# A mixture-of-experts loop written as one fixed cycle per pair of experts

## The chip, the cores and the metric

The kernel is one program on one core of a Trainium2 chip. TensorE (PE) multiplies matrices and loads its stationary operand in a separate stage (PEld); VectorE (DVE), ScalarE (ACT) and GpSimd (POOL) do elementwise work; SyncE (SP) issues the weight transfers from DRAM, which 16 DMA engines carry out. SBUF is the on-chip store, PSUM holds matmul results. The metric is the device time of one execution in microseconds (us), as the median of several runs.

## The reference

Two transformer blocks over 256 tokens of width 1024. The first ends in a mixture of 32 experts; the second (adaptive norms, a Hyena long convolution beside differential attention, a feed-forward layer) is not touched by the change. The part that matters, cut down:

```python
def block_ffn(args):                       # one block of rows of one expert
    tok, e = args
    xb = xt[tok]
    hb = jax.nn.silu(xb @ w1[e]) * (xb @ w3[e])      # 1024 -> 512
    return hb @ w2[e]                                # 512 -> 1024
...
y = jnp.einsum('nk,nkd->nd', gate, y_assign)         # each token: 2 of 32 experts
```

The Hyena filters of the second block do not depend on the tokens: a small two-layer network with sines (f1, f2), its output layer times a decay (f3), and its Fourier transform (fH), for each of two orders n.

## The kernel before, in words

The tokens of each expert are gathered by a matmul with a 0/1 matrix: up to 64 tokens for an expert, two experts (a *pair*) side by side in 128 columns. `NJ` is 16 pairs. For pair j the loop (L1303 to L1332) makes these pieces of work, whose names and lines are those of the profile:

- `up(j, "w1")` and `up(j, "w3")` (L1266): 16 products each into a PSUM tile `hw`. A product is 64 rows of stationary tokens by 512 columns of weights; the two experts of a pair use the two halves of PE's columns ("half-column products"), alternating. The first 8 of 16 read kb 0 of the weight, the last 8 read kb 1.
- `act_half` (L1271): SiLU on ACT into `sg`; at L1325 DVE multiplies `sg` by the w3 result.
- `turn` (L1277): four 128x128 transposes of `sg` into `tp`, and ACT copies them to `hT` (L1279).
- `down(j)` (L1296): 16 half-column products of `hT` with w2, into `po0` and `po1`.
- `combine` (L1014): scales `po` by the gates and splits it in a high part `oth` (ACT, L237) and a low part `otl` (DVE, L238); eight full-width products `py` scatter the rows back to the tokens; DVE adds each of four results to `x` (L1016).
- `gather` (L936, L937): 8 blocks per group of two pairs, each of 4 products `pxg` and an ACT copy into `xg`; the loop takes 2 + 2 blocks in each pair up to pair 13.
- `hooks`: at pair 6 `filters` sets up the Hyena filter work, at pairs 7 to 14 one filter step each (f1, f2, f3(0), fH(0,0), fH(0,1), f3(1), fH(1,0), fH(1,1) with the inverse), at pair 15 `wide_ring`.

Each pair needs 12 weight loads of 1 MiB (4 of w1, 4 of w3, 4 of w2; L1231, the last w2 in halves at L1292), 192 MiB in all. SP issues them in program order into a ring of SBUF buffers (`wtile`): a load waits until the products of the load that had its buffer before are done. The ring has 16 buffers until pair 6. There `filters` gives ten of them up and adds two, so that 8 are left, after the w1 loads of pair 6; at pair 15 three are added.

In the code of before, the w3 products come in two parts: w3 kb 0, then `down(j-1)`, then two gather blocks, then w3 kb 1; `turn` of the pair before stands right behind w1. But the code's order is not the order on PE: a list scheduler of the language orders each engine's instructions by priority and by when it takes them to be ready, so that pieces of neighbouring steps are interleaved. PSUM holds three sets of tiles: `acc` has 4 tiles (`hw1`, `hw3`, `po0`, `po1`), `tp` two and `sm` two; `py` uses two of each, and before the change all gather blocks use `sm`.

Of the kernel before, what the change touches and what calls it, by code (L numbers as in the profile page):

```python
# [100 lines left out]

def _body(nc, tc, I, out, ctx, dbg):
    V, A, G, T = nc.vector, nc.scalar, nc.gpsimd, nc.tensor

    cst = ctx.enter_context(tc.tile_pool(name="cst", bufs=1))
    NA = 4
# [816 lines left out]
    def gather(iot, d1, d2, xg):  # L923


        hot = wk.tile([P, 2, 256], F32R, name="hot", tag="junk", bufs=1)
        for t in range(2):
            hit = wk.tile([P, S], F32, name="hit", tag="tb", bufs=1)
            V.tensor_scalar(hit, iot, d1[:, t:t + 1], None, op0=OP.is_equal)
            V.scalar_tensor_tensor(hot[:, t, :], iot, d2[:, t:t + 1], hit, op0=OP.is_equal, op1=OP.add)  # L930

        def block(k):
            p = smp("pxg")[:, :256]
            for t in range(2):
                for z_ in range(2):
                    T.matmul(p, xn[z_][:, t, k * P:(k + 1) * P], hot[:, t, :], start=t + z_ == 0, stop=t + z_ == 2)  # L936
# [50 lines left out]
    def bc_rows(dst, src):  # L987
        p = smp("prow")
        for k in range(2):
            for t in range(2):  # L990
                T.matmul(p[:, k * S + t * P:k * S + (t + 1) * P], src[:, k, t:t + 1].to_broadcast([P, P]), ident,
                         start=True, stop=True)
        V.tensor_copy(dst, p.rearrange("p (k s) -> p k s", k=2))

    def combine(rw, sid, po, done=None):

        ET = wk.tile([P, S], F32R, name="ET", tag="wh", bufs=4)
        tmp = wk.tile([P, S], F32, name="ETt", tag="tb", bufs=1)
        gs = mo.tile([P, 2], F32, name="gs", tag="gs", bufs=4)
        V.tensor_scalar(tmp, rw[:, 0, :], sid, None, op0=OP.is_equal)  # L1000
        V.scalar_tensor_tensor(ET, rw[:, 1, :], sid, tmp, op0=OP.is_equal, op1=OP.add)
        for k in range(2):
            V.scalar_tensor_tensor(tmp, rw[:, k, :], sid, rows[:, 1, k, :], op0=OP.is_equal, op1=OP.mult,
                                   accum_out=gs[:, k:k + 1])
        V.tensor_tensor(gs[:, 0:1], gs[:, 0:1], gs[:, 1:2], op=OP.add)
        hl = []
        for hf in range(2):
            hl.append([wk.tile([P, 512], F32R, name=n_, tag=g_, bufs=4) for n_, g_ in (("oth", "wh"), ("otl", "wl"))])
            hilo(*hl[hf], po[hf], gs[:, 0:1])
        for t in range(2):  # L1010
            for hf in range(2):
                p = smp("py") if t == 0 else tpp("py")
                for z_ in range(2):
                    T.matmul(p, ET[:, t * P:(t + 1) * P], hl[hf][z_], start=z_ == 0, stop=z_ == 1)  # L1014
# [13 lines left out]
    def overflow(n_over):  # L1028
        with tc.If(n_over > 0):  # L1029
# [34 lines left out]
            with tc.For_i(0, n_over, 1):  # L1064
# [17 lines left out]
                for st in range(2):  # L1082
                    A.activation(sgs[st], hps[0][st], AF.Silu)
                    V.tensor_tensor(sgs[st], sgs[st], hps[1][st], op=OP.mult)
                    p = tpp()
                    for q in range(4):
                        T.transpose(p[:, q * P:(q + 1) * P], sgs[st][:, q * P:(q + 1) * P], ident)
# [26 lines left out]
    def lambdas():  # L1114
        V.tensor_tensor(lv[:, 0:2, :], lv[:, 0:2, :], lv[:, 2:4, :], op=OP.mult)
        ls = mo.tile([1, 2], F32, name="ls")
        V.tensor_reduce(ls, lv[:, 0:2, :], AX.X, OP.add)
        A.activation(ls, ls, AF.Exp)
        V.scalar_tensor_tensor(ls[:, 0:1], ls[:, 0:1], 0.2, ls[:, 1:2], op0=OP.add, op1=OP.subtract)
        p = smp("lam")  # L1120
        T.matmul(p[:, 0:1], ones[0:1, :], ls[:, 0:1], start=True, stop=True)
        V.tensor_copy(lam, p[:, 0:1])

    def filters():
# [37 lines left out]
        def inverse():  # L1162

            hilo(*dfs, dft)
            for ri in range(2):
                p = tpp()
                for fb_ in range(2):
                    for t in range(2):
                        T.transpose(p[:, fb_ * S + t * P:fb_ * S + (t + 1) * P], dft[:, ri, t, fb_ * P:(fb_ + 1) * P], ident)
                A.activation(inv[:, ri], p.rearrange("p (b s) -> p b s", b=2), AF.Copy, scale=(1 - 2 * ri) / 256.0)  # L1170

        def f1():
            p = smp("f1")
            T.matmul(p[0:64, :S], w1, zT, start=True, stop=True)
            h1 = st["h1"] = fp.tile([64, S], F32, name="fh1")
            sin_of(h1, p[0:64, :S], fb[:, 0:1], fb[:, 2:3])

        def f2():
            p = smp("f2")
            T.matmul(p[0:64, :S], w2, st["h1"], start=True, stop=True)  # L1180
            h2 = st["h2"] = fp.tile([65, S], F32, name="fh2")
            sin_of(h2[0:64, :], p[0:64, :S], fb[:, 1:2], fb[:, 2:3])
            V.memset(h2[64:65, :], 1.0)

        def f3(n):
# [3 lines left out]
            for t in range(2):  # L1189
                for d_ in range(2):  # L1190
                    p = smp("f3")
                    T.matmul(p, st["h2"][:, t * P:(t + 1) * P], w3[:, d_ * 512:(d_ + 1) * 512], start=True, stop=True)
# [7 lines left out]
        def fH(n, ri):  # L1200
            src = st["src"][ri]
            for fb_ in range(2):
                p = smp("fH")
                for t in range(2):
                    T.matmul(p, dft[:, ri, t, fb_ * P:(fb_ + 1) * P], src[:, t, :], start=t == 0, stop=t == 1 and ri == 1)  # L1205
                if ri == 0:

                    for k in range(4):
                        T.matmul(p[:, k * P:(k + 1) * P], col["hy_bias_2"][:, 4 * n + k:4 * n + k + 1].to_broadcast([P, P]),
                                 ident, start=False, stop=k == 3)  # L1210
# [49 lines left out]
    def up(j, nm, hps, kbs):  # L1260
        s0 = (j % 2) * P
        for kb in kbs:
            we = [eload(nm, 2 * j + e, kb, 4, 512) for e in range(2)]
            for k in range(4):
                for e in range(2):
                    T.matmul(hps[64 * e:64 * e + 64, :], xgs[j][:, 4 * kb + k, s0 + 64 * e:s0 + 64 * e + 64], we[e][:, k, :],  # L1266
                             start=kb + k == 0, stop=kb + k == 4)

    def act_half(hps):
        sg = wk.tile([P, 512], F32, name="sg", tag="wl", bufs=4)  # L1270
# [3 lines left out]
    def turn(sg):  # L1274
        p = tpp()
        for q in range(4):
            T.transpose(p[:, q * P:(q + 1) * P], sg[:, q * P:(q + 1) * P], ident)  # L1277
# [4 lines left out]
    def down(j, hT):  # L1282
        po = [acc("po0"), acc("po1")]
        for kb in range(2):
# [8 lines left out]
            for q in range(2):  # L1293
                for hf in range(2):
                    for e in range(2):
                        T.matmul(po[hf][64 * e:64 * e + 64, :], hT[:, 2 * kb + q, 64 * e:64 * e + 64],  # L1296
                                 we[e][:, q, hf * 512:(hf + 1) * 512], start=kb + q == 0, stop=kb + q == 2)
# [6 lines left out]
    prev = None  # L1304
    for j in range(NJ):
        if j == 2:
            combine(rows[:, 0], slotc[:, 1:2], down(1, turn(prev)))
            prev = None
            overflow(n_over)
        if j % 2 == 0 and j + 2 < NJ:  # L1310
# [15 lines left out]
        if j == 0:  # L1326
            n_over = nc.values_load(novi[0:1, 0:1], min_val=0, max_val=7)
            bc_rows(rows[:, 0], dest)
            bc_rows(rows[:, 1], gt)
# [4 lines left out]
    combine(rows[:, 0], slotc[:, NJ - 1:NJ], down(NJ - 1, turn(prev)), norm_part)  # L1334
    tap("x3", x)
    moctx.close()

# [317 lines left out]
```

## Time and profile before

| | before |
|---|---|
| median of 3 runs | 1326.5 us (1323.0 to 1326.77) |
| the profiled execution, own time | 1325.16 us |
| its span (first to last instruction) | 1323.3 us |
| mean granted PE clock, share of full | 0.993 |
| PE busy | 1277.0 us (97%) |
| DVE, ACT, POOL busy | 747.7, 552.6, 69.3 us |
| the expert stage, from its first weights to the last `po` | about 388 to 880 us of the span |

Busy means that an instruction of that engine is under way; for PE the ends are modelled, and a wait for the weights inside a row of products is not always seen as idle. DMA share is the mean busy share of the 16 DMA engines.

### The profile page before, as it was taken

Reading aid. Unit: us, or ns where it says so; the run is one execution under the profiler, and the core shown is the slowest. Engines: PE = TensorE matmul, PEld = TensorE weight load, DVE = VectorE, ACT = ScalarE, POOL = GpSimd, SP = SyncE. Lnnn points to the kernel's source line nnn. Section 1 sums busy time; section 2 is a strip of 40 time slices with the busy share of each in tenths; the row PEclk is TensorE's granted clock in tenths of the full one; section 3 lists DMA queues with packets and bytes.
Section 4 is the critical chain, followed back from the end, with each engine's and each line's share of the span. In section 5 each row is a group of like instructions: output and inputs, shape, how many; then the busy total and the mean of one; then the engine's idle time right before and its main releaser. Section 6 shows DMA issues by size and latency. Waiting matters only on the chain.

```text
span 1323.3 us, 18184 instructions
## 1 busy us (share of the span) xinstructions
PE 1277.0 (97%) x6920; PEld 884.8 (67%) x6920; DVE 747.7 (57%) x1474; ACT 552.6 (42%) x1016; POOL 69.3 (5%) x118
## 2 busy tenths in 40 slices
PE   7999999999999999999999999969999999999996
PEld 7988788998874433333333333329887996799985
DVE  6986888756752321222321411258898678667654
ACT  6867555755641111111111111036346556455542
POOL 1101000100000000100000000010000101000000
PEclk9999999999999999999999999999999999999999
DMA  9755775994459999699999999977543576576751
GB/s 346 256 197 175 263 250 178 388 337 159 140 187 421 419 421 420 255 422 420 409 396 354 383 379 350 421 289 249 196 155 117 193 215 214 177 238 195 225 186 48
DMA packets 103242, 365.27 MB, mean 276 GB/s; under 512 B 6840, under 2 KB 9203, under 8 KB 78960
## 3 DMA queue, kind: packets, MB, share of 16 engines
q1 hardware_dynamic: 93264, 329.77, 67.0%
q0 software_dynamic: 9744, 34.18, 7.5%
q8 instruction: 55, 0.90, 0.3%
q14 instruction: 35, 0.29, 0.1%
q10 hardware_dynamic: 144, 0.14, 0.0%
HBM read 363.00 MB, written 1.06 MB: 275 GB/s over the span
## 4 chain that ended last, share of the span: by engine, by line
PE 56%; DMA 3%; DVE 3%; issue 2%; ACT 2%; POOL 1%; DVEq 0%; POOLq 0%; ACTq 0%
PE hw L1266 16%; PE po L1296 6%; PE acc L345 5%; PE acc L344 5%; PE acc L346 5%; PE acc L310 2%; PE acc L309 2%; PE acc L308 2%; PE pxg L936 2%; PE py L1014 2%; DMA w<-in_w_dram 2%; PE fH L1205 1%; PE iy L1420 1%; PE s L1462 1%; DMA w<-in_w_ffn_gate_dram 1%
## 5 line engine op out<-in xcount | busy, mean ns | idle before, releaser
L296 ACT ACTIVATE wh<-w 128x512 fp32r<-128x512 f32 (+1 forms) x454 | 278.8, 622 | 241.0 <-PE acc L310 105.9
L297 DVE TENSOR_TENSOR wl<-w,wh 128x512 fp32r<-128x512 f32 (+1 forms) x454 | 302.6, 682 | 134.6 <-ACT wh L296 132.3
L1266 PE MATMUL hw<-w,xg 128*64 128x512 f32 x1024 | 258.0, 598 | 1.8 <-DVEq L1029 1.8
L238 DVE SCALAR_TENSOR_TENSOR otl<-po,gs,oth 128x512 fp32r<-128x512 f32 x32 | 23.9, 749 | 294.6 <-ACT oth L237 293.9
L1266 PEld LDWEIGHTS hw<-w,xg 128*64 128x64 f32 x1024 | 75.2, 136 | 147.1 <-issue 141.9
L1296 PE MATMUL po<-w,hT 128*64 128x512 f32 x512 | 128.8, 594 | 2.5 <-ACT hT L1279 1.5
L1296 PEld LDWEIGHTS po<-w,hT 128*64 128x64 f32 x512 | 42.2, 137 | 77.7 <-issue 69.4
L344 PE MATMUL acc<-xfh,wh 128*128 128x256 f32 x288 | 81.1, 282 | 0.0
L345 PE MATMUL acc<-xfl,wh 128*128 128x256 f32 x288 | 81.1, 282 | 0.0
L346 PE MATMUL acc<-xfh,wl 128*128 128x256 f32 x288 | 81.0, 281 | 0.0
L237 ACT ACTIVATE oth<-po,gs 128x512 fp32r<-128x512 f32 x32 | 21.9, 688 | 139.5 <-PE po L1296 130.8
L450 DVE SCALAR_TENSOR_TENSOR junk<-waT,cb 128x1024 bf16<-128x1024 f32 x64 | 78.0, 1219 | 3.7 <-DMA waT<-in_l_waT_dram 3.4
L309 PE MATMUL acc<-wl,xmh 128*128 128x512 f32 x192 | 76.7, 399 | 0.8 <-DVE wl L297 0.7
L310 PE MATMUL acc<-wh,xml 128*128 128x512 f32 x192 | 76.3, 397 | 0.0
L308 PE MATMUL acc<-wh,xmh 128*128 128x512 f32 x192 | 75.8, 399 | 0.0
L937 ACT ACTIVATE xg<-pxg,vec 128x256 f32<-128x256 f32 x64 | 30.1, 474 | 104.0 <-PE pxg L936 102.8
L345 PE MATMUL acc<-x2l,wh 128*128 128x256 f32 x224 | 64.0, 288 | 0.5 <-DVE x2l L244 0.5
L344 PE MATMUL acc<-x2h,wh 128*128 128x256 f32 x224 | 64.0, 290 | 0.3 <-ACT x2h L282 0.3
L346 PE MATMUL acc<-x2h,wl 128*128 128x256 f32 x224 | 64.1, 287 | 0.0
L345 PEld LDWEIGHTS acc<-xfl,wh 128*128 128x128 f32 x288 | 54.2, 188 | 0.0
L346 PEld LDWEIGHTS acc<-xfh,wl 128*128 128x128 f32 x288 | 54.2, 188 | 0.0
L344 PEld LDWEIGHTS acc<-xfh,wh 128*128 128x128 f32 x288 | 54.2, 188 | 0.0
(542 smaller groups left out, 2528.9 us busy)
## 6 DMA issues: line engine op xcount, KB each, us to landing
w<-in_w_dram SPq DMA_DIRECT2D x188, 1024.0 KB, 10.4
w<-in_w_in_dram SPq DMA_DIRECT2D x54, 1024.0 KB, 6.7
waT<-in_l_waT_dram POOLq DMA_DIRECT2D x48, 512.0 KB, 5.1
w<-in_w_ffn_gate_dram SPq DMA_DIRECT2D x10, 1024.0 KB, 5.4
w<-in_w_ffn_up_dram SPq DMA_DIRECT2D x10, 1024.0 KB, 5.3
w<-in_w_ffn_down_dram SPq DMA_DIRECT2D x10, 1024.0 KB, 5.3
w<-in_w_out_dram SPq DMA_DIRECT2D x8, 1024.0 KB, 5.3
w<-in_w_xkv_dram SPq DMA_DIRECT2D x8, 1024.0 KB, 14.2
```

The costliest lines, as they stand in the source:

```text
L296: last["act"] = A.activation(h[:, :n], w, AF.Copy)
L297: last["dve"] = V.tensor_tensor(l[:, :n], w, f(h[:, :n]), op=OP.subtract)
L308: T.matmul(p, xh[:, k, s], h[:, :n], start=k == 0, stop=False)
L309: T.matmul(p, xh[:, k, s], l[:, :n], start=False, stop=False)
L310: T.matmul(p, xl[:, k, s], h[:, :n], start=False, stop=k == KB - 1)
L344: T.matmul(p, h[:, s], xh[:, k, :], start=k == 0 and b % 2 == 0, stop=False)
L345: T.matmul(p, h[:, s], xl[:, k, :], start=False, stop=False)
L346: T.matmul(p, l[:, s], xh[:, k, :], start=False, stop=k == KB - 1 and b in (nb - 1, b // 2 * 2 + 1))
L450: V.scalar_tensor_tensor(junk(), w[i_][:, b, :], 1.0, cb[:, r_, :], op0=OP.mult, op1=OP.mult, accum_out=adac[:, n, r_:r_ + 1])
L937: A.activation(xg[:, k, :], p, AF.Copy, scale=col["l_gmoe"][:, k:k + 1])
L1266: T.matmul(hps[64 * e:64 * e + 64, :], xgs[j][:, 4 * kb + k, s0 + 64 * e:s0 + 64 * e + 64], we[e][:, k, :], start=kb + k == 0, stop=kb + k ...
L1296: T.matmul(po[hf][64 * e:64 * e + 64, :], hT[:, 2 * kb + q, 64 * e:64 * e + 64], we[e][:, q, hf * 512:(hf + 1) * 512], start=kb + q == 0, ...
```

## The change

The loop is rewritten as one cycle: all w1 products, all of `down(j-1)`, all w3 products, then `combine(j-1)`, all four gather blocks, the filter step if there is one, and the transposes of this pair (`turn` moves from the next pair's cycle to the end of its own). Each piece is opened with `pe_after()`, which tells the scheduler that PE instructions inside come behind the last PE instruction traced so far (`traced` keeps it). That sets the order of issue on PE and makes no wait of its own. Two smaller things come with it: gather blocks alternate between the `tp` and `sm` PSUM tiles, and `lambdas` (a few small instructions) moves from the start of pair 0 to behind its w3 products. Nothing is computed otherwise: the instructions on every engine are the same ones.

```diff
         def block(k):
-            p = smp("pxg")[:, :256]
+            p = (tpp if k % 2 else smp)("pxg")[:, :256]
...
+    class pe_after:
+
+        def __enter__(self):
+            self.c = tc.issue_after(traced[-1].ins) if traced else ExitStack()
+            return self.c.__enter__()
...
         h1 = acc("hw1")
-        up(j, "w1", h1, (0, 1))
-        hT = turn(prev) if prev is not None else None
+        with pe_after():
+            up(j, "w1", h1, (0, 1))
         sg = act_half(h1)
-        if j in hooks:
+        if j in (6, 15):
             hooks[j]()
+        po = None
+        if hT is not None:
+            with pe_after():
+                po = down(j - 1, hT)
         h3 = acc("hw3")
-        up(j, "w3", h3, (0,))
-        po = down(j - 1, hT) if hT is not None else None
-        gather_some(2)
-        up(j, "w3", h3, (1,))
+        with pe_after():
+            up(j, "w3", h3, (0, 1))
         V.tensor_tensor(by_row(sg, 4), by_row(sg, 4), in_block(h3, 4), op=OP.mult)
...
         if po is not None:
-            combine(rows[:, 0], slotc[:, j - 1:j], po)
-        gather_some(2)
-        prev = sg
+            after_down(j - 1, po)
+        with pe_after():
+            gather_some(4)
+        if 6 < j < 15 and j in hooks:
+            with pe_after():
+                hooks[j]()
+        with pe_after():
+            hT = turn(sg)
```

**PE at the end of a plain pair (pair 4).** `hw_5018` is the w3 result of pair 4 and `hw_5126` the w1 result of pair 5; rows are PE's instructions in order. Before:

```order
L1014 MATMUL py<-oth,ET 128x512
L1014 MATMUL py<-otl,ET 128x512
L1266 MATMUL hw_5018<-w,xg 64x512
L1014 MATMUL py<-otl,ET 128x512
L1014 MATMUL py<-oth,ET 128x512
...
L1266 MATMUL hw_5018<-w,xg 64x512 x7
...
L1266 MATMUL hw_5126<-w,xg 64x512
L1277 MATMUL tp<-ca,sg 128x128 x4
L936 MATMUL pxg<-hot,xnl 128x256
L1266 MATMUL hw_5126<-w,xg 64x512 x15
L1266 MATMUL hw_5160<-w,xg 64x512 x8
```

The same pair after; `hw_5044` is its w3 result, `hw_5133` the w1 result of pair 5, `po_5018` and `po_5019` the results of `down(3)`:

```order
L1268 MATMUL hw_4991<-w,xg 64x512 x16
L1298 MATMUL po_5018<-w,hT 64x512
...
L1298 MATMUL po_5019<-w,hT 64x512 x2
L1268 MATMUL hw_5044<-w,xg 64x512 x16
L1016 MATMUL py<-oth,ET 128x512
L1016 MATMUL py<-otl,ET 128x512
...
L938 MATMUL pxg<-hot,xnh 128x256
L938 MATMUL pxg<-hot,xnl 128x256
L1279 MATMUL tp<-ca,sg 128x128 x4
L1268 MATMUL hw_5133<-w,xg 64x512 x16
```

Before, one product of the w3 half stands alone among the `py`, and one of the next w1 alone ahead of the transposes; after, the half-column products of a pair stand in one row of 48, and everything of full width behind them in another.

**PE at a filter step (pair 10, fH(0,0)).** `hw_5820` is the w3 result of that pair and `hw_5938` the w1 result of the next. Before:

```order
L1205 MATMUL fH<-hsm,dft 128x512
L1266 MATMUL hw_5820<-w,xg 64x512 x7
L1205 MATMUL fH<-hsm,dft 128x512
L1266 MATMUL hw_5938<-w,xg 64x512
L1277 MATMUL tp<-ca,sg 128x128 x4
L1209 MATMUL fH<-ca,vec 128x128 x4
L1205 MATMUL fH<-hsm,dft 128x512
L1266 MATMUL hw_5938<-w,xg 64x512 x8
L1205 MATMUL fH<-hsm,dft 128x512
L1209 MATMUL fH<-ca,vec 128x128 x4
```

After (`hw_6103` is the next w1 result):

```order
L938 MATMUL pxg<-hot,xnl 128x256
L1207 MATMUL fH<-hsm,dft 128x512 x2
L1211 MATMUL fH<-ca,vec 128x128 x4
L1207 MATMUL fH<-hsm,dft 128x512 x2
L1211 MATMUL fH<-ca,vec 128x128 x4
L1279 MATMUL tp<-ca,sg 128x128 x4
L1268 MATMUL hw_6103<-w,xg 64x512 x16
```

The step stood in pieces between half-column products of two pairs, and now stands in one piece ahead of the transposes.

**SP's loads of one pair, after.** In the code of before, the four w2 loads stood between the two w3 halves; now they stand ahead of all four w3 loads:

```order
L1233 DMA w_4992<-in_w1_dram 128x2048
L1233 DMA w_4994<-in_w1_dram 128x2048
L1233 DMA w_5004<-in_w1_dram 128x2048
L1233 DMA w_5006<-in_w1_dram 128x2048
L1233 DMA w_5020<-in_w2_dram 128x2048
L1233 DMA w_5022<-in_w2_dram 128x2048
L1233 DMA w_5032<-in_w2_dram 128x2048
L1233 DMA w_5034<-in_w2_dram 128x2048
L1233 DMA w_5045<-in_w3_dram 128x2048
L1233 DMA w_5047<-in_w3_dram 128x2048
L1233 DMA w_5057<-in_w3_dram 128x2048
L1233 DMA w_5059<-in_w3_dram 128x2048
```

So the order of loads still is the order in which PE uses them.

## Rows read from the trace of the kernel before

**Rows 1.** Windows: us, busy PE PEld DVE ACT POOL, PEclk, DMA share, GB/s

```profile
388.00:880.00 492.00, 482.26 (x2072) 187.13 (x2070) 127.77 (x281) 74.86 (x134) 4.86 (x9) 1.00 0.97 390
893.00:1323.30 430.30, 413.05 (x2672) 368.55 (x2672) 313.11 (x587) 225.59 (x420) 28.71 (x50) 0.98 0.57 185
```

**Rows 2.** Windows inside the expert stage, same columns

```profile
395.00:511.50 116.50, 113.80 (x531) 46.58 (x530) 27.14 (x64) 17.55 (x33) 0.00 (x0) 1.00 1.01 420
511.50:540.00 28.50, 28.45 (x125) 11.01 (x124) 6.30 (x14) 4.36 (x8) 3.26 (x6) 1.00 0.96 385
540.00:570.90 30.90, 30.40 (x126) 11.66 (x124) 9.69 (x21) 5.99 (x10) 0.54 (x1) 1.00 0.71 278
570.90:631.00 60.10, 59.44 (x252) 23.23 (x252) 18.38 (x47) 8.76 (x18) 0.00 (x0) 1.00 1.01 421
...
631.00:835.00 204.00, 200.58 (x826) 76.50 (x825) 52.56 (x106) 31.56 (x56) 0.52 (x1) 1.00 0.96 380
664.30:700.00 35.70, 35.64 (x149) 14.07 (x148) 8.24 (x18) 5.57 (x11) 0.00 (x0) 1.00 0.99 393
835.00:862.80 27.80, 26.97 (x125) 10.52 (x124) 7.68 (x16) 2.61 (x5) 0.00 (x0) 1.00 1.01 420
```

**Rows 3.** Timeline of PE, pair 4: start, us, what (two records per product)

```profile
513.92 1.07 PE L1266 MATMUL hw<-w,xg 128*64 128x512 f32 x2
...
515.73 0.28 PE L936 MATMUL pxg<-hot,xnh 128*128 128x256 f32 x1
...
517.48 3.65 PE L1266 MATMUL hw<-w,xg 128*64 128x512 f32 x14
...
521.72 1.07 PE L1266 MATMUL hw<-w,xg 128*64 128x512 f32 x2
522.72 0.66 PE L1277 MATMUL tp<-ca,sg 128*128 128x128 f32 x4
```

**Rows 4.** Timeline of PE around pair 1 and 2, same columns

```profile
427.32 3.65 PE L1266 MATMUL hw<-w,xg 128*64 128x512 f32 x16
430.90 0.50 PE L1014 MATMUL py<-oth,ET 128*128 128x512 f32 x1
...
432.87 0.28 PE L936 MATMUL pxg<-hot,xnh 128*128 128x256 f32 x1
...
446.55 10.52 PE L1266 MATMUL hw<-w,xg 128*64 128x512 f32 x48 [1.85 <-DVEq L1029]
```

**Rows 5.** The chain that ended last, pair 4: start, us, what

```profile
511.51 0.70 ACT oth L237
...
512.23 0.76 DVE otl L238
```

**Rows 6.** The same chain, filter steps

```profile
642.74 1.72 PE f L1192 x4
...
677.11 0.89 PE fH L1209 x8
...
820.91 1.02 PE tp L1169 x8
```

**Rows 7.** Groups by line, 470 to 530 us: busy us, mean ns

```profile
L1016 DVE TENSOR_TENSOR x<-py,x 128x512 f32<-128x512 f32 x8 | 5.1, 684 | 0.7 <-PE py L1014 0.7
L937 ACT ACTIVATE xg<-pxg,vec 128x256 f32<-128x256 f32 x10 | 4.7, 473 | 23.1 <-PE pxg L936 22.8
L1325 DVE TENSOR_TENSOR sg<-sg,hw 128x512 f32<-128x512 f32 x2 | 1.4, 686 | 3.2 <-PE hw L1266 3.2
```

**Rows 8.** Waits of SP's queue, 380 to 900 us: total us, times, longest

```profile
SPq L1231 <- PE hw L1266: 291.2, 100, 15.7
SPq L1231 <- PE po L1296: 93.8, 49, 15.0
```

**Rows 9.** Timeline of SP where the ring gets smaller: issue of two loads

```profile
554.54 1.17 SPq L1231 DMA_DIRECT2D w<-in_w_dram  x2
```

**Rows 10.** DMA issues of the whole program: count, KB, us from issue to landing

```profile
w<-in_w_out_dram SPq DMA_DIRECT2D x8, 1024.0 KB, 5.3
```

More of the change, by code (lines that the diff above doesn't have):

```diff
@@ L103, in _body @@
     V, A, G, T = nc.vector, nc.scalar, nc.gpsimd, nc.tensor
+    traced = []
     cst = ctx.enter_context(tc.tile_pool(name="cst", bufs=1))
@@ L990, in bc_rows @@
             for t in range(2):
-                T.matmul(p[:, k * S + t * P:k * S + (t + 1) * P], src[:, k, t:t + 1].to_broadcast([P, P]), ident,
-                         start=True, stop=True)
+                traced[:] = [T.matmul(p[:, k * S + t * P:k * S + (t + 1) * P], src[:, k, t:t + 1].to_broadcast([P, P]), ident,
+                            start=True, stop=True)]
         V.tensor_copy(dst, p.rearrange("p (k s) -> p k s", k=2))
@@ L1086, in overflow @@
                     for q in range(4):
-                        T.transpose(p[:, q * P:(q + 1) * P], sgs[st][:, q * P:(q + 1) * P], ident)
+                        traced[:] = [T.transpose(p[:, q * P:(q + 1) * P], sgs[st][:, q * P:(q + 1) * P], ident)]
                     for q in range(2):
@@ L1120, in lambdas @@
         p = smp("lam")
-        T.matmul(p[:, 0:1], ones[0:1, :], ls[:, 0:1], start=True, stop=True)
+        traced[:] = [T.matmul(p[:, 0:1], ones[0:1, :], ls[:, 0:1], start=True, stop=True)]
         V.tensor_copy(lam, p[:, 0:1])
@@ L1173, in f1 @@
             p = smp("f1")
-            T.matmul(p[0:64, :S], w1, zT, start=True, stop=True)
+            traced[:] = [T.matmul(p[0:64, :S], w1, zT, start=True, stop=True)]
             h1 = st["h1"] = fp.tile([64, S], F32, name="fh1")
@@ L1179, in f2 @@
             p = smp("f2")
-            T.matmul(p[0:64, :S], w2, st["h1"], start=True, stop=True)
+            traced[:] = [T.matmul(p[0:64, :S], w2, st["h1"], start=True, stop=True)]
             h2 = st["h2"] = fp.tile([65, S], F32, name="fh2")
@@ L1204, in fH @@
                 for t in range(2):
-                    T.matmul(p, dft[:, ri, t, fb_ * P:(fb_ + 1) * P], src[:, t, :], start=t == 0, stop=t == 1 and ri == 1)
+                    traced[:] = [T.matmul(p, dft[:, ri, t, fb_ * P:(fb_ + 1) * P], src[:, t, :], start=t == 0, stop=t == 1 and ri == 1)]
                 if ri == 0:
                     for k in range(4):
-                        T.matmul(p[:, k * P:(k + 1) * P], col["hy_bias_2"][:, 4 * n + k:4 * n + k + 1].to_broadcast([P, P]),
-                                 ident, start=False, stop=k == 3)
+                        traced[:] = [T.matmul(p[:, k * P:(k + 1) * P], col["hy_bias_2"][:, 4 * n + k:4 * n + k + 1].to_broadcast([P, P]),
+                                    ident, start=False, stop=k == 3)]
                 A.activation(Hf[:, n, ri, fb_, :], p, AF.Copy)
@@ L1265, in up @@
                 for e in range(2):
-                    T.matmul(hps[64 * e:64 * e + 64, :], xgs[j][:, 4 * kb + k, s0 + 64 * e:s0 + 64 * e + 64], we[e][:, k, :],
-                             start=kb + k == 0, stop=kb + k == 4)
+                    traced[:] = [T.matmul(hps[64 * e:64 * e + 64, :], xgs[j][:, 4 * kb + k, s0 + 64 * e:s0 + 64 * e + 64], we[e][:, k, :],
+                                start=kb + k == 0, stop=kb + k == 4)]
     def act_half(hps):
@@ L1276, in turn @@
         for q in range(4):
-            T.transpose(p[:, q * P:(q + 1) * P], sg[:, q * P:(q + 1) * P], ident)
+            traced[:] = [T.transpose(p[:, q * P:(q + 1) * P], sg[:, q * P:(q + 1) * P], ident)]
         hT = wk.tile([P, 4, P], F32, name="hT", tag="wl", bufs=4)
@@ L1295, in down @@
                     for e in range(2):
-                        T.matmul(po[hf][64 * e:64 * e + 64, :], hT[:, 2 * kb + q, 64 * e:64 * e + 64],
-                                 we[e][:, q, hf * 512:(hf + 1) * 512], start=kb + q == 0, stop=kb + q == 2)
+                        traced[:] = [T.matmul(po[hf][64 * e:64 * e + 64, :], hT[:, 2 * kb + q, 64 * e:64 * e + 64],
+                                    we[e][:, q, hf * 512:(hf + 1) * 512], start=kb + q == 0, stop=kb + q == 2)]
         return po
@@ L1302, in gather_some, with __exit__, after_down @@
             todo.pop(0)()
-    prev = None
+    class pe_after:
+        def __enter__(self):
+            self.c = tc.issue_after(traced[-1].ins) if traced else ExitStack()
+            return self.c.__enter__()
+        def __exit__(self, *a):
+            return self.c.__exit__(*a)
+    hT = None
+    def after_down(j, po, done=None):
+        with pe_after():
+            combine(rows[:, 0], slotc[:, j:j + 1], po, done)
     for j in range(NJ):
         if j == 2:
-            combine(rows[:, 0], slotc[:, 1:2], down(1, turn(prev)))
-            prev = None
+            with pe_after():
+                po = down(1, hT)
+            with pe_after():
+                gather_some(2)
+            after_down(1, po)
+            hT = None
+            traced.clear()
             overflow(n_over)
+            traced.clear()
         if j % 2 == 0 and j + 2 < NJ:
@@ L1314, in _body @@
         h1 = acc("hw1")
-        up(j, "w1", h1, (0, 1))
-        hT = turn(prev) if prev is not None else None
+        with pe_after():
+            up(j, "w1", h1, (0, 1))
         sg = act_half(h1)
-        if j in hooks:
+        if j in (6, 15):
             hooks[j]()
+        po = None
+        if hT is not None:
+            with pe_after():
+                po = down(j - 1, hT)
         h3 = acc("hw3")
-        up(j, "w3", h3, (0,))
-        po = down(j - 1, hT) if hT is not None else None
-        gather_some(2)
-        up(j, "w3", h3, (1,))
+        with pe_after():
+            up(j, "w3", h3, (0, 1))
         V.tensor_tensor(by_row(sg, 4), by_row(sg, 4), in_block(h3, 4), op=OP.mult)
         if j == 0:
+            lambdas()
             n_over = nc.values_load(novi[0:1, 0:1], min_val=0, max_val=7)
-            bc_rows(rows[:, 0], dest)
-            bc_rows(rows[:, 1], gt)
+            with pe_after():
+                bc_rows(rows[:, 0], dest)
+                bc_rows(rows[:, 1], gt)
         if po is not None:
-            combine(rows[:, 0], slotc[:, j - 1:j], po)
-        gather_some(2)
-        prev = sg
-    combine(rows[:, 0], slotc[:, NJ - 1:NJ], down(NJ - 1, turn(prev)), norm_part)
+            after_down(j - 1, po)
+        with pe_after():
+            gather_some(4)
+        if 6 < j < 15 and j in hooks:
+            with pe_after():
+                hooks[j]()
+        with pe_after():
+            hT = turn(sg)
+    with pe_after():
+        po = down(NJ - 1, hT)
+    after_down(NJ - 1, po, norm_part)
     tap("x3", x)
```

8 lines of the change are left out of this document (4 added, 4 removed).

## The prediction

> **What bounds the kernel now.** I read the windows by stage first, to see which resource is full in the stage that the change rewrites; then the same windows pair by pair, to see where it is not full; then PE's timeline and the chain in one pair, for the price of the order; last the waits of SP's queue, for what holds a load up.
>
> The expert stage takes 492 us and moves 390 GB/s at a DMA share of 0.97; PE is busy for 482 of it, at the full granted clock of 1.00, the 2.4 GHz level [rows 1]. So two resources are nearly full, and the question is which one is the bound where. The windows inside answer it [rows 2]. From 395 to 511 us the loads run at 420 GB/s and a share of 1.01, and from 570.9 to 631 us at 421: that is what the loads can do, and these stretches are bound by them. At 421 GB/s one load (1 MiB, 1.0486 MB) takes 2.49 us, the 12 of a pair 29.9 us. From 511.5 to 570.9 us, where the ring of buffers gets smaller, the rate falls to 385 and then 278 GB/s. In the six pairs with big filter steps (631 to 835 us) it is 380: there a pair takes 204.0/6 = 34.0 us, over the 29.9 that its loads need, and PE is busy for 200.6 of 204.0. So PE binds these pairs.
>
> If the loads ran at 421 GB/s throughout, the stage would be 492 x (1 - 390/421) = 36 us shorter. No order on PE can give back more than that. After the stage nothing is altered: the 430 us behind it stay [rows 1].
>
> **The change part by part.**
>
> *A half-column product that stands alone.* Eight products take 3.65 us [rows 4], and seven take 3.65 as well [rows 3]: two neighbours run side by side in the two halves of PE's columns, and the seventh's partner is the one that stands alone, at 1.07 us, of which the chain sees 1.0 until its successor starts. There are two such products in a plain pair [rows 3], both gone after the change: 2.0 us. The plain pair of the trace (511.5 to 540) takes 28.5 us [rows 2].
>
> *The wait for the split.* Before, the first `py` comes right behind the last `po` and waits for 0.70 us of ACT and 0.76 of DVE [rows 5]; part of it is filled, and about 0.8 shows. After, a whole w3 of 16 products stands between them: about 7 us of cover, so the wait goes. What is late next is PSUM: gather block 1 takes the tile of the third `py`, which the third addition to `x` must release. DVE first multiplies `sg` (0.69 us), then adds at 0.68 each [rows 7]: 0.69 + 3 x 0.68 = 2.7 us behind w3's end, while PE is there after 1.97 of `py` and one block of 0.6. Between 0 and 1.2 us, I take 0.7 by those rows (with about 0.6 for releases and starts).
>
> *The plain pair after.* 48 half-column products are two rows of 24 at 10.52, 21.0 us; eight `py` 432.87 - 430.90 = 1.97 us, call it 1.9 [rows 4]; 16 `pxg` between 1.9 (four ACT copies of 0.473 [rows 7]) and 2.5 (11 took 1.75 [rows 3]), I take 2.3; the PSUM wait 0.7; transposes 0.66 [rows 3]. Sum 26.6 us, against 28.5: 1.9 less (2.0 + 0.8 - 0.7 by parts gives 2.1; I keep the smaller).
>
> A break in a row of half-column products shows in rows as 2 x 3.65 - 7.09, or (3 x 3.65 - 10.52)/2: about 0.2 us [rows 3, 4]. The lone products' 1.0 us holds its own breaks already, so the sum has no further term for it. The page TensorEngine Tiling (Array Packing), Key Properties, of the Trainium skill says that PE drains when its tiling mode changes, which before happens eight times in a plain pair and after twice; by that, priced apart from the lone products, an estimated 6 x 0.2 = 1.2 us a pair would come on top, of which the loads' floor lets at most 3 us through in the filter pairs: 30.6 in place of the 27.6 below.
>
> *The filter pairs.* A step of four big products costs 4 x 0.86 = 3.44 us (two take 1.72), fH(n,0) 2 x 0.89 = 1.78 more [rows 6]. f3 and fH(0,1) make 26.6 + 3.44 = 30.0, fH(n,0) 31.8 (it was 35.7 [rows 2]). Pair 14 has no gather (less 2.3 and 0.7) but the inverse's eight transposes, 1.02 [rows 6], and copies between them that I put at 0.7: 28.8. Six pairs: 30.0 + 31.8 + 30.0 + 30.0 + 31.8 + 28.8 = 182.4 us. The loads alone need 6 x 29.9 = 179.4, so PE still binds here, and the gain is 204.0 - 182.4 = **21.6 us**.
>
> *The load-bound stretches.* PE's 26.6 or so is under the loads' 29.9: a faster PE only waits for its weights. 570.9 to 631 us stays (0). Before pair 6 PE runs behind the loads, with up to 16 in flight or held, so being faster brings it forward: that is paid out at the ring change.
>
> *The ring change.* Two windows there lose 28.5 x (1 - 385/421) = 2.4 and 30.9 x (1 - 278/421) = 10.5 us of load time, 12.9 in all [rows 2]. The loads stand still because the small ring's first buffers are still to be read; the next two go out at 554.54, with the w1 products of pair 6 [rows 9]. PE gets there earlier by the four plain pairs 2 to 5 at 1.9 and about one lone product more, 8 us. Some stall stays, since giving up half the ring leaves eight loads ahead where there were up to 16. Gain **8 us**, bounds 3 (if PE meets its weights first) and 12.9.
>
> *The last pair.* It takes 27.8 us now [rows 2], because PE comes out of the filter pairs with loads in stock; after, the loads bind it, 29.9: **-2 us**. The sum: 21.6 + 8 - 2 = 27.6 us.
>
> *The cover of the filter step.* The ring of eight must bridge the stretch in which PE frees no buffer: `py`, `pxg`, wait, transposes, which is 5.6 us, 9.0 with f3, 10.8 with fH(n,0). The first buffers come free about 3.5 us into the next row of products (eight products read two loads [rows 4]), and a load issued then takes 5.3 us to land when nothing is queued [rows 10]: 14.4, 17.8 and 19.6 us. Eight loads are 8 x 2.49 = 19.9 us. So it costs nothing, but only just; this is the part that I trust least. The waits on `hw` products (100 of them, up to 15.7 us) and on `po` (49) [rows 8] show that SP's loads do wait for PE's releases now.
>
> Other edits. Loads keep the order of their use. `lambdas` and `bc_rows` sit in pair 0, in stretches covered by loads: 0. The other hooks (6 and 15) stay.
>
> All this is against the profiled execution's 1325.2 us: 1297.6. The median is 1.3 higher, so **1299 us**.
>
> **The rivals.**
>
> *A, a thinner cover.* If only six of the eight buffers are really ahead (14.9 us), because two are always under PE's hands, f3-like pairs lose 17.8 - 14.9 = 2.9 and fH(n,0) 4.7, in all 3 x 2.9 + 2 x 4.7 and about 1 = 19 us. Gain 9, 1317 us. For it: loads are issued two at a time as a pair of experts ends. Against: the window at 664.3 runs at 393 GB/s now, with a step in it [rows 2].
>
> *B, slower.* The same mechanism further on: each cycle ends in one long stretch that frees nothing, and with a cover of five loads (12.5 us) pairs 7, 8 and 15 lose 2.0 each, three f3-like pairs 5.4, two with fH(n,0) 7.1 and pair 14 about 2.4: 39 us, against 27.6 gained: 11 slower, 1337 us. It decides at about 5.6 loads. For it: before, products are sprinkled through the step and release buffers all along. Against: eight buffers, and 5.3 us to land.
>
> *C, the same.* The share is 0.97 already; if the dips of 385 and 380 GB/s are the transfers' own and not PE's, the saving turns into waits for weights: 1322 to 1326 us. Against: 1.01 and 421 as soon as PE keeps up.
>
> For C there is also a rule of the skill. DMA: Bandwidth & Descriptors, Specifications, of the Trainium skill gives about 358 GB/s of HBM bandwidth for one core. By it 201.3 MB of weights would need an estimated 562 us, the stage would be at its floor and the time the same; the measured 420 GB/s [rows 2] is above that, as the page's own single-core figure of 425 is, so it does not bind here.
>
> That the change does not do what it says is left out: the order of issue shows the row of 48 in every pair.
>
> **How the numbers follow.** Forecast 0.70, A (and values up to 1321) 0.12, C 0.07, B 0.09, a gain beyond the ceiling, with other stages moved, 0.02. The forecast's own terms run from 21.6 + 12.9 - 0 = 34.5 (1292), with the 36 of the ceiling 1290, to about 15 + 3 - 2 = 16 (1310), where the filter pairs lose 1 us each. The range must leave out no more than 2 in 10: 1288 to 1318 us takes in the forecast and most of A. 0.3% is 4 us, about what a measurement of this kernel can tell from no change. Faster: 0.70 + 0.12 + 0.02 = 0.84; same 0.07; slower 0.09.
>
> **What the profile after would show.** Right: PE rows of 48 half-column products (96 records) in about 21 us and no row of 1.07 us; filter pairs of 30 to 32 us; 415 GB/s or more from 630 us on; the dip at the ring change at about 5 us; the last `po` near 852 us instead of 880; the PE clock at 1.00. Wrong: loads standing still at the end of each cycle with waits of `hw` on `w` of 3 us or more behind the transposes (A, B); pairs of 34 us with the loads at 380 GB/s and PE waiting (C). What would break the sum is above all the time from a buffer's release to the landing of its next load under full queues.

## The result, and the profile after

The changed kernel takes 1294.4 us (median of 4 runs, 1292.7 to 1296.3) beside 1325.4 us of the kernel before (4 runs): a ratio of 0.9769, 95% interval 0.9756 to 0.9781, or 31 us less. The profiled execution took 1296.29 us, its span 1294.6 us. The forecast was 1299 us, the range 1288 to 1318.

Windows of the changed kernel come first, in the columns of [rows 1]: the whole expert stage, then the stretches that answer to [rows 2]: a plain pair, the ring change, pairs 7 and 8, the six pairs with big filter steps, one of them alone (pair 11, fH(0,1)), and the rest of the program.

```profile
388.00:849.84 461.84, 443.41 (x2073) 197.40 (x2071) 127.29 (x282) 76.09 (x135) 4.88 (x9) 1.00 1.01 415
511.50:537.66 26.16, 26.02 (x129) 12.65 (x129) 5.51 (x10) 5.11 (x10) 3.81 (x7) 1.00 1.02 414
537.66:569.74 32.08, 28.73 (x126) 11.78 (x125) 10.41 (x26) 5.03 (x10) 0.00 (x0) 1.00 1.02 408
569.74:630.91 61.17, 55.34 (x254) 23.61 (x253) 16.58 (x41) 9.35 (x17) 0.00 (x0) 1.00 1.01 421
630.91:815.93 185.02, 180.10 (x820) 82.22 (x819) 54.06 (x113) 30.78 (x55) 0.53 (x1) 1.00 1.01 414
697.34:725.99 28.65, 28.65 (x134) 13.28 (x133) 8.17 (x18) 5.56 (x11) 0.00 (x0) 1.00 0.98 402
...
862.00:1294.60 432.60, 415.24 (x2672) 370.34 (x2672) 313.21 (x587) 225.55 (x420) 28.86 (x50) 0.98 0.56 184
```

Read the last column downwards. Before, it fell to 385, 278 and 380 GB/s in three stretches [rows 2]; now the three that answer to them have 414, 408 and 414 (a single filter pair 402), and the stage as a whole moves 415 at a share of 1.01. PE is busy for 443 of 462 us, at the granted clock of 1.00 as before: the engine that was the bound in half of the stage now has time to spare in nearly every pair, and the loads have hardly any. The last `po` ends at 849.84, where it was 880 [rows 1], 30 us earlier. From there to the end of the span it is 444.8 us, against 443.3 before.

PE's timeline in pairs 4 and 5 of the changed kernel (start, us, what, two records for each half-column product) shows the cycle:

```profile
507.42 0.50 PE L1016 MATMUL py<-oth,ET 128*128 128x512 f32 x1
...
509.38 0.29 PE L938 MATMUL pxg<-hot,xnh 128*128 128x256 f32 x1
...
511.56 0.66 PE L1279 MATMUL tp<-ca,sg 128*128 128x128 f32 x4
512.14 7.09 PE L1268 MATMUL hw<-w,xg 128*64 128x512 f32 x32
519.06 7.09 PE L1298 MATMUL po<-w,hT 128*64 128x512 f32 x32
525.92 7.09 PE L1268 MATMUL hw<-w,xg 128*64 128x512 f32 x32
532.94 0.50 PE L1016 MATMUL py<-oth,ET 128*128 128x512 f32 x1
...
537.66 7.49 PE L1268 MATMUL hw<-w,xg 128*64 128x512 f32 x32
```

From w1 to w1 it is 537.66 - 512.14 = 25.5 us, against 28.5 in [rows 2]. The 48 half-column products run from 512.14 to 532.94 without a gap, no row of 1.07 us as in [rows 3] is left here or anywhere in the stage, and `py` follows w3 at once: the wait of [rows 5] is gone, and in this pair no wait for PSUM has taken its place.

A little later, in pair 6, PE waits for weights. The bracket at a row's end is idle time ahead of it and what ended that:

```profile
556.47 3.65 PE L1268 MATMUL hw<-w,xg 128*64 128x512 f32 x16 [1.28 <-DMA w<-in_w_dram]
```

Over the whole stage these waits are the largest of PE (total us, times, longest):

```profile
PE hw L1268 <- DMA w<-in_w_dram: 12.9, 11, 1.9
PE hw L1268 <- DVEq L1031: 1.8, 1, 1.8
```

### The profile page after: what moved, and what is told of

It reads as the page before. It is cut to its first block, busy times and chain, and to the rows that moved or that the text cites. A ratio compares the mean times of both kernels' runs of the same rounds, so it can differ in the third digit from the quotient of the medians.

```text
span 1294.6 us, 18193 instructions
## 1 busy us (share of the span) xinstructions
PE 1240.6 (96%) x6920; PEld 897.6 (69%) x6920; DVE 747.9 (58%) x1474; ACT 552.5 (43%) x1016; POOL 70.2 (5%) x118
## 4 chain that ended last, share of the span: by engine, by line
PE 50%; DMA 9%; issue 3%; DVE 2%; ACT 1%; POOL 1%; SPq 0%; DVEq 0%; POOLq 0%; ACTq 0%
PE hw L1268 13%; DMA w<-in_w_dram 7%; PE acc L347 5%; PE acc L346 5%; PE acc L348 5%; PE po L1298 3%; PE acc L312 2%; PE acc L311 2%; PE acc L310 2%; PE py L1016 2%; PE pxg L938 1%; PE iy L1454 1%; PE fH L1207 1%; PE s L1496 1%; DMA w<-in_w_ffn_gate_dram 1%
## 5 line engine op out<-in xcount | busy, mean ns | idle before, releaser
L1268 PE MATMUL hw<-w,xg 128*64 128x512 f32 x1024 | 234.8, 595 | 14.8 <-DMA w<-in_w_dram 12.9
L1268 PEld LDWEIGHTS hw<-w,xg 128*64 128x64 f32 x1024 | 79.3, 137 | 154.6 <-issue 127.2
L1298 PE MATMUL po<-w,hT 128*64 128x512 f32 x512 | 120.0, 595 | 2.2 <-ACT hT L1281 1.5
L939 ACT ACTIVATE xg<-pxg,vec 128x256 f32<-128x256 f32 x64 | 29.6, 476 | 139.3 <-PE pxg L938 139.0
L1350 DVE TENSOR_TENSOR sg<-sg,hw 128x512 f32<-128x512 f32 x16 | 11.0, 689 | 106.5 <-PE hw L1268 106.5
## 6 DMA issues: line engine op xcount, KB each, us to landing
w<-in_w_dram SPq DMA_DIRECT2D x188, 1024.0 KB, 13.6
```

The source lines that it names most:

```text
L1268: traced[:] = [T.matmul(hps[64 * e:64 * e + 64, :], xgs[j][:, 4 * kb + k, s0 + 64 * e:s0 + 64 * e + 64], we[e][:, k, :], start=kb + k == 0 ...
L1298: traced[:] = [T.matmul(po[hf][64 * e:64 * e + 64, :], hT[:, 2 * kb + q, 64 * e:64 * e + 64], we[e][:, q, hf * 512:(hf + 1) * 512], start= ...
```

## The experiments

Two theories were to be told apart. **T**, that of the prediction: PE's cycle got shorter, by products that no longer stand alone and rows that are no longer broken, until the loads became the bound. **R**: the order and release of the loads is what pays (w2 ahead of w3, buffers freed in one row), whatever PE's time. The other rivals concern single parts: all half-column products together, the filter step in one piece, the second set of PSUM tiles, the ring's cover. Ratios are against the kernel before, taken on the same chip.

**The tie alone taken away.** The source stays in its new order, but nothing is tied:

```diff
-            self.c = tc.issue_after(traced[-1].ins) if traced else ExitStack()
+            self.c = ExitStack()
```

> The changed source with the order left to the scheduler (no piece is tied behind the one before). It then places lone half-column products among the full-width ones again. Theory T (PE's cycle is shorter because no product stands alone and no row is broken): most of the gain goes, 1315 to 1328 us. Rival R (the new order of loads and of the source is what pays, not PE's order): 1294 to 1300 us.

Measured: 1309.5 us, ratio 0.9890 (0.9869 to 0.9911). Neither number was met: half of the gain stays. The order of its instructions tells why. In a plain pair the scheduler again puts one product of w3 alone among the `py`. The transposes, which follow the third row below, now cut the first product of w1 off from the others: it stands at the end of a row of nine (18 records), which takes 4.50 us where eight take 3.65. The pair takes 532.27 - 503.69 = 28.6 us from `py` to `py`, as before:

```profile
503.69 0.73 PE L1016 MATMUL py<-oth,ET 128*128 128x512 f32 x2
...
505.38 1.07 PE L1268 MATMUL hw<-w,xg 128*64 128x512 f32 x2
...
513.30 4.50 PE L1268 MATMUL hw<-w,xg 128*64 128x512 f32 x18
...
532.27 0.74 PE L1016 MATMUL py<-oth,ET 128*128 128x512 f32 x2
```

But in the filter pairs less is broken. In pair 10 the kernel before cuts w3 and the next w1 around the step, and three products stand alone there (at 666.8, 675.5 and 688.9 us); the w1 lies in pieces of 1, 8 and 7 products. Untied, w3 is still cut into 1, 8 and 7, but the next w1 stands whole behind the transposes, as two rows of the timeline show:

```profile
701.66 0.60 PE L1279 MATMUL tp<-ca,sg 128*128 128x128 f32 x4
702.19 7.09 PE L1268 MATMUL hw<-w,xg 128*64 128x512 f32 x32
```

So, read from this trace, the source's new order alone repairs a good part of the filter pairs, and the tie repairs the plain ones. The expectation took it for granted that the scheduler would fall back to the old order.

**The old places, tied.** The source's order of before, each piece tied behind the one before it:

```diff
+            with pe_after():
+                hT = turn(prev)
...
+            up(j, "w3", h3, (0,))
         if hT is not None:
             with pe_after():
                 po = down(j - 1, hT)
...
+            gather_some(2)
+        with pe_after():
+            up(j, "w3", h3, (1,))
```

> The order of the source of before (w1, transposes, filter step, first half of w3, down, two gather blocks, second half of w3, combination, two gather blocks), but each piece tied behind the one before. No product stands alone, yet the half-column products stand in three rows in place of one. T: two more breaks of about 0.2 us in each pair, 0.4 x 6 in the pairs that PE binds: 1297 us (1294 to 1301). Rival (all half-column products together is what counts): 1310 us or more.

Measured: 1292.0 us, ratio 0.9757 (0.9735 to 0.9779), not to be told from the change itself. Its timeline has three rows in a pair, none with a lone product:

```profile
510.52 0.50 PE L1016 MATMUL py<-oth,ET 128*128 128x512 f32 x1
...
513.90 7.09 PE L1268 MATMUL hw<-w,xg 128*64 128x512 f32 x32
520.92 0.66 PE L1279 MATMUL tp<-ca,sg 128*128 128x128 f32 x4
521.50 3.65 PE L1268 MATMUL hw<-w,xg 128*64 128x512 f32 x16
524.99 7.09 PE L1298 MATMUL po<-w,hT 128*64 128x512 f32 x32
...
533.15 3.65 PE L1268 MATMUL hw<-w,xg 128*64 128x512 f32 x16
536.73 0.50 PE L1016 MATMUL py<-oth,ET 128*128 128x512 f32 x1
```

All half-column products in one row is therefore not what counts. A fixed order without lone products is enough. The two breaks more make PE's cycle 536.73 - 510.52 = 26.2 us in place of 25.5, and nothing of that can be measured in the time. It has the loads' old order and places too, so it speaks against R.

**Two products alone again.** The changed kernel, with two products of the next w1 put back between full-width work:

```diff
+            with pe_after():
+                one(j + 1, *nxt, 0, 0)
         with pe_after():
             gather_some(4)
...
+                one(j + 1, *nxt, 1, 0)
         with pe_after():
             hT = turn(sg)
```

> As the changed kernel, but two products of the next w1 stand alone again, one ahead of the gather blocks and one ahead of the transposes, in pairs 2 to 14. T: 2.0 us more of PE in every pair; it shows in the six pairs with big filter steps, which have little slack, and not in the plain ones, where the loads are the bound: 1303 us (1299 to 1308). Rival R (order of loads and release of buffers): 1294 us, no change.

Measured: 1304.1 us, ratio 0.9856 (0.9835 to 0.9878), the time that T gave. The timeline shows both rows, and the first `py` of two pairs in a row, 538.86 - 511.39 = 27.5 us apart, where the changed kernel has 532.94 - 507.42 = 25.5:

```profile
511.39 0.50 PE L1016 MATMUL py<-oth,ET 128*128 128x512 f32 x1
...
513.44 1.07 PE L1273 MATMUL hw<-w,xg 128*64 128x512 f32 x2
...
516.53 1.07 PE L1273 MATMUL hw<-w,xg 128*64 128x512 f32 x2
...
538.86 0.50 PE L1016 MATMUL py<-oth,ET 128*128 128x512 f32 x1
```

Two lone products cost 2.0 us of PE in each of 13 pairs, 26 us, of which 10 reach the end; the rest is covered by loads. But they do not reach it only through the filter pairs, as the expectation had it. Windows of this run:

```profile
511.50:570.00 58.50, 55.42 (x248) 23.45 (x248) 15.93 (x35) 9.55 (x17) 3.81 (x7) 1.00 0.92 373
631.00:816.00 185.00, 183.27 (x807) 80.85 (x807) 53.98 (x113) 30.79 (x55) 0.53 (x1) 1.00 0.99 403
```

The changed kernel moves 410 and 414 GB/s in the same windows. At 421 GB/s as the loads' full rate, that is 5.1 us more of load time lost at the ring change and 4.8 more in the filter pairs: PE's slower plain pairs are paid for where the ring gets smaller.

**The loads' old order alone.** `down` between the two halves of w3, everything else as in the change:

```diff
+            up(j, "w3", h3, (0,))
+        if hT is not None:
+            with pe_after():
+                po = down(j - 1, hT)
+        with pe_after():
+            up(j, "w3", h3, (1,))
```

> As the changed kernel, but down stands between the two halves of w3, so that the loads come in the order of before (w1, half of w3, w2, half of w3); the row of 48 half-column products stays. T: no change, 1292 to 1297 us. Rival R (the order of loads pays): 1302 us or more.

Measured: 1294.4 us, ratio 0.9777 (0.9745 to 0.9809): no change. R falls: the loads' old order costs nothing here, nor with the old places tied, where buffers also come free in three rows, and two lone products cost 10 us at the new order of loads.

**The filter steps at their old place, not tied.**

```diff
-        if j in (6, 15):
+        if j in hooks and j:
             hooks[j]()
...
-        if 6 < j < 15 and j in hooks:
-            with pe_after():
-                hooks[j]()
```

> As the changed kernel, but the filter steps of pairs 7 to 14 stand where they stood before and are not tied. Their products then break the w1 row into 9 and 7. T: about 1.3 us more in six pairs, less some slack: 1299 us (1296 to 1304). Rival (bringing the filter step into one piece is most of the gain): 1310 us or more.

Measured: 1295.6 us, ratio 0.9790 (0.9769 to 0.9810), a little under what was expected and not to be told from the change, whose interval this one overlaps. Its w1 row is cut into 9 and 7 in these pairs, and PE has the time for it: from 631 to 816 us it is busy for 184.8 of 185.0 us, against 180.1 in the changed kernel, and the loads run at 413 GB/s, against 414. Bringing the step into one piece is not needed once the rest is tied.

**One set of PSUM tiles for the gather.**

```diff
-            p = (tpp if k % 2 else smp)("pxg")[:, :256]
+            p = smp("pxg")[:, :256]
```

> As the changed kernel, but all gather blocks use the one set of two PSUM tiles as before. T: at most 0.4 us of waits for ACT's copies in each pair, hidden under the loads in most: 1293 to 1297 us. Rival (the second set of PSUM tiles is a good part of the gain): 1302 us or more.

Measured: 1293.6 us, ratio 0.9766 (0.9741 to 0.9792): no change.

**Seven, six and nine buffers.** The buffers that `filters` adds to the ring, two in the change:

```diff
-        change_ring([wpC] * 2, (wpB,))
+        change_ring([wpC], (wpB,))
```

With `[]` there are six; for nine the pool has three, and `fh1` shares the place of `hsm`.

> As the changed kernel, with seven buffers in place of eight after pair 6. The cover is 7 x 2.49 = 17.4 us; the stretch without a release plus 8.8 us is 13.5 in a plain pair, 17.0 with four big filter products and 18.8 with fH(n,0). T: two stalls of 1.4 us and 2.5 us at the ring change: 1299 us (1295 to 1303). Rival (the cover is thinner than its count, rival A of the prediction): 1308 us or more.

> As the changed kernel, with six buffers in place of eight after pair 6: a cover of 14.9 us. T: stalls of about 2.1 us in four pairs and 3.9 us in two, and 5 us at the ring change: 1315 us (1307 to 1322). If the cover is thinner than its count: 1330 us or more. If the buffers do not matter: 1294 us.

> The changed kernel with nine buffers in place of eight after pair 6 (the room comes from a small filter tile that shares a larger one's place); the order on every engine is the same. T: the changed kernel's loads already follow each other with hardly a gap, so a ninth buffer has about 2 us to give: 1291 to 1295 us, ratio to the kernel before 0.975 to 0.978. Rival (the cover is still thin: from six to seven buffers gave 14 us, from seven to eight 9 us, so the ninth gives 4 to 5 more): 1290 us or less, ratio 0.974 or less.

Measured: seven 1303.6 us, ratio 0.9839 (0.9811 to 0.9866); six 1317.3 us, ratio 0.9939 (0.9919 to 0.9960); nine 1292.4 us, ratio 0.9761 (0.9743 to 0.9778). The step from eight to seven costs 9 us, where I expected 5, the next one 14, and a ninth buffer gives nothing that can be told from noise. The same window of each kernel, six, seven and nine buffers in that order:

```profile
631.00:816.00 185.00, 170.68 (x751) 73.42 (x750) 48.23 (x99) 27.98 (x51) 0.52 (x1) 1.00 0.90 367
```

```profile
631.00:816.00 185.00, 174.54 (x790) 76.89 (x788) 51.03 (x108) 28.58 (x51) 0.53 (x1) 1.00 0.97 396
```

```profile
631.00:816.00 185.00, 180.60 (x825) 83.19 (x826) 54.06 (x113) 31.35 (x56) 0.53 (x1) 1.00 1.01 418
```

The chain that ended last shows the mechanism (start, us, what). With seven buffers, and in the next filter pairs alike, the first half of `down` frees a buffer, SP issues the next load into it, and the second half of w3 waits until that has landed:

```profile
704.03 3.46 PE po L1298 x16
707.49 8.97 DMA w<-in_w_dram
...
716.50 3.65 PE hw L1268 x14
```

With six it is the same, and longer:

```profile
708.61 3.48 PE po L1298 x16
...
712.49 11.16 DMA w<-in_w_dram
...
723.70 3.65 PE hw L1268 x14
```

From release to landing it takes 9.0 and 11.2 us, not the 5.3 of [rows 10] that the cover's sum had used. Those 5.3 us belong to the loads of another weight; the page of the kernel before has 10.4 us for the loads of the expert weights themselves:

```profile
w<-in_w_dram SPq DMA_DIRECT2D x188, 1024.0 KB, 10.4
```

With seven buffers the loads nearly stand still at 700 us, where SP waits for products to free a buffer, and run at full rate all through the 9.0 us:

```profile
700.00:702.00 2.00, 2.00 (x12) 0.71 (x10) 0.00 (x0) 0.00 (x0) 0.00 (x0) 1.00 0.45 82
707.50:716.50 9.00, 7.68 (x34) 2.70 (x31) 1.50 (x2) 1.37 (x2) 0.00 (x0) 1.00 1.01 426
```

At 426 GB/s these 9.0 us move 3.7 MiB, so other loads are queued ahead of the one that PE waits for. That fits a buffer less being dearer than I expected.

**Fewer bytes.** Half of each w2 load is left out, in the changed kernel and in the one before; products use the first 512 columns twice, so the result is another, and the instructions of PE, DVE and ACT are as many as they were.

```diff
-                we = [eload("w2", 2 * j + e, kb, 2, 1024) for e in range(2)]
+                we = [wtile(2, 1024) for e in range(2)]
+                for e in range(2):
+                    nc.sync.dma_start(we[e][:, :, 0:512], erows("w2", 2 * j + e, kb * 2, 2)[:, :, 0:512])
```

> The changed kernel with half of each w2 load left out (its products use the first 512 columns twice; all instructions of PE, DVE and ACT are the same). Loads of a pair then need 24.9 us. T (the loads bind the changed stage nearly throughout): PE alone decides, 25.5 us in a plain pair: about 23 us less, 1271 us (1266 to 1280). Rival (PE or a wait on another engine still binds): 1288 us or more.

> The kernel before with the same half of each w2 load left out. T: PE binds it in the plain pairs too, at 28.5 us, and the stall at the ring change goes in part: about 9 us less, 1316 us (1309 to 1320); the distance to the changed kernel with the same loads left out grows to about 45 us, which is PE's own saving. Rival R (loads and releases are what the change mends): the distance shrinks below 31 us.

Measured (two runs each): the changed kernel 1272.7 us, ratio 0.9602 (0.9559 to 0.9645); the kernel before 1310.3 us, ratio 0.9886 (0.9853 to 0.9918). PE's waits for weights in the changed kernel's stage (to 829 us) fall from 12.9 us to

```profile
PE hw L1268 <- DMA w<-in_w_dram: 1.6, 2, 1.3
```

So the loads do bind the changed stage. With them nearly out of the way (the kernel before shows no wait of PE for weights in its stage) the two kernels stand 37.6 us apart, not the 45 that I had worked out, but more than 31: PE's own saving is larger than what the change gives, and some 7 us of it are under the loads.

**Products by expert.** In w1 and w3, four products of one expert and then four of the other, in place of alternating.

```diff
-            for k in range(4):
-                for e in range(2):
+            for e in range(2):
+                for k in range(4):
```

> The changed kernel with the w1 and w3 products of one load and expert in a row (four of one expert, then four of the other, in place of alternating). T (a half-column product is cheap only beside one of the other half): eight products take about 6 to 7 us in place of 3.65, 10 to 13 us more in each pair, 1460 to 1500 us. Rival (a lone product is dear because of the change of shape around it): 3.65 us as before, 1294 us.

Measured, one run: 1314.1 us. Neither number was met, and T's size was wrong by far: a plain pair takes 27.6 us from `py` to `py` in place of 25.5, 2.1 us more and not 10 to 13. The timeline at the end of w1:

```profile
495.55 7.68 PE L1268 MATMUL hw<-w,xg 128*64 128x512 f32 x29
502.65 0.64 PE L1298 MATMUL po<-w,hT 128*64 128x512 f32 x1
503.07 0.59 PE L1268 MATMUL hw<-w,xg 128*64 128x512 f32 x1
...
503.93 0.59 PE L1268 MATMUL hw<-w,xg 128*64 128x512 f32 x1
503.99 6.12 PE L1298 MATMUL po<-w,hT 128*64 128x512 f32 x26
```

Products of `po` have begun in one half of the columns while three records of w1, one and a half products, are still to come in the other. So a half-column product does not need its partner next to it in the order: four places away is enough for most of the overlap. That a product alone costs 1.0 us because full-width work on both sides leaves it no partner fits these rows and those of the two lone products; no run tests that by another edit.

## Why the prediction was right, step by step

**PE binds the filter pairs, and the loads are the floor.** Right. The loads' time that was lost can be read off the windows before and after, by the prediction's own rule (1 - rate/421):

| stretch | lost before | lost after | gain | forecast |
|---|---|---|---|---|
| ring change | 12.9 us [rows 2] | 26.16 x (1 - 414/421) + 32.08 x (1 - 408/421) = 1.4 | 11.5 | 8 |
| six filter pairs | 204 x (1 - 380/421) = 19.9 [rows 2] | 185.02 x (1 - 414/421) = 3.1 | 16.8 | 21.6 |
| whole stage | 36 [rows 1] | 461.84 x (1 - 415/421) = 6.6 | 29.6 | 27.6 |

The last row answers to the 30 us by which the last `po` is earlier.

**The plain pair.** 26.6 us forecast, 25.5 measured. The term of 0.7 us for PSUM was not there: `pxg` follows `py` without a gap. The rest is a shorter row of `pxg` (509.38 to 511.56, 2.2) and 20.8 in place of 21.0 for the row of 48. The price of a lone product, 1.0 us, was confirmed by putting two back (2.0 us).

**The ring change.** The mechanism was right, the term mis-sized: 8 us taken of a possible 12.9, 11.5 measured. PE arrives in pair 6 early enough that almost no stall is left, and waits up to 1.3 us at a time for weights there.

**The filter pairs.** 182.4 us forecast, 185.0 measured, so 19.0 us less by the windows' lengths, and 16.8 by the loads. PE's own part was, if anything, shorter than forecast (28.65 us in pair 11, forecast 30.0). What was missing in the sum, which had PE still binding these pairs, is that PE comes into pairs 9 and 10 with no weights in stock: 4.0 of its 4.5 us of waits for w in these six pairs fall there, the two take 33.6 and 32.7 us where 30.0 and 31.8 were forecast, and the loads, at 414 GB/s over the six, set the pace. Two signs named for this part were narrowly missed: the pairs take 28.1 to 33.6 us, not 30 to 32, and the loads run at 414 GB/s, not 415 or more.

**The last pair.** The loads do not bind it: from 816 us to the end of the stage PE shows no wait for w, and w1, `down` and w3 follow each other as fast as anywhere (815.93 to 838.64 us, with 1.8 us of other products between), so the reason given for the -2 us was wrong. As load time the term belongs to the filter pairs, whose 21.6 us were more than the 19.9 that they had lost; the two terms together are 19.6, and 16.8 were measured.

**The total.** It came out closer than its terms, and that is luck: the ring change gave 3.5 us more than its 8, the filter pairs and the last pair 2.8 less than their 19.6.

**The cover.** "It costs nothing, but only just": right in both parts. Nine buffers give nothing more, seven cost 9 us. The sum behind it was not sound: with the 9.0 us measured in place of 5.3 it comes to 21.5 us with f3 and 23.3 with fH(n,0), over the 19.9 of eight loads, and yet PE's waits for w in pairs 11 to 14, each behind such a step, are 0, 0.2, 0.3 and 0 us. So the outcome was right and the sum was lucky. Rival A's price for a cover of six, 1317 us, is what six buffers give, 1317.3, in part by chance: A took off 19 us of the forecast gain, and six buffers cost 22.9 of the measured one. Its mechanism is real, and the changed kernel meets it with one buffer less. Rival B did not occur; C falls with the 414 and 408 GB/s where the dips had been, and with the bytes taken out.

**The breaks beyond the lone products.** The page TensorEngine Tiling (Array Packing), Key Properties, of the Trainium skill says that a change of the tiling mode drains TensorE. The prediction's estimate by that, 0.2 us a change, would make 0.8 us a pair for the kernel with three rows, which changes mode six times in a pair where the change does it twice. Its cycle of 26.2 us against 25.5 is near that, 0.7 us; some 0.4 of it lie at the gather blocks, where this trace does not part a change of mode from a wait for ACT's copies. The loads hide it: that kernel is as fast as the change.

**Not settled.** How the gain of the untied order (15 us) divides between the filter pairs and the ring change was read from one trace and not tried part by part. By the rule above, its 362 GB/s from 511.5 to 570 us and 405 from 631 to 816 make 4.7 us at the ring change and 12.9 in the filter pairs, a little more together than was measured. The move of `lambdas` was undone in no run; it lies in pair 0, in stretches where the loads run at 420 GB/s both before and after.

## What to carry to other kernels

When a list scheduler interleaves narrow and full-width matmuls, count in its order the narrow ones that stand alone or are cut off from their partner: two per cycle were 2.0 us of 28.5 here, and tying the pieces, in either order, took them out. Before counting a gain on an engine that is nearly full, work out what the next nearly full resource leaves of it: 37.6 us of PE's time were saved, and 31 arrived. When a cycle is rearranged so that buffers come free in bursts, test the ring one buffer smaller and one larger: a flat side and a steep side of 9 us show how near the edge it is.

## What had not been expected of the hardware

The two halves of PE's columns run apart from each other by several products: with four products of one half ahead of four of the other, the cycle of 25.5 us grew by 2.1, where by the estimate made ahead of that run a need for strict neighbours would have cost 10 to 13. A load issued while others are queued took 9.0 us to land in the kernel with seven buffers and 11.2 in that with six, and the median of the expert weights' loads is 13.6 us in the changed kernel and 10.4 in the one before, against 5.3 for the loads of [rows 10].
